# A hybrid decoder step: sums of the norms on one engine, the convolution's mean behind each tile, and a later write of the next layer's input

## The chip, the cores and the metric

The kernel runs on one core of one Trainium2 chip. A core has five engines that run side by side, each with its own in-order queue: TensorE (PE: matmul, with its weight loads shown as PEld), VectorE (DVE), ScalarE (ACT), GpSimd (POOL) and SyncE (SP, which here only issues DMAs). The metric is the device time of one execution in microseconds (us). Lower is better.

## The reference

One inference step of a two-layer decoder with width 1024: a prompt of 1024 tokens with 16 meta tokens ahead of it, and eight decode sequences of one token each. Layer 0 mixes tokens with a causal Conformer convolution, layer 1 with a recurrent mixer (RWKV-7). Each is followed by an MLP with 4096 hidden features. All is float32.

```python
hn  = rmsnorm(h, norm_mix[i])
# layer 0
u   = hn @ w_pw1 + b_pw1;  u = u[:D] * sigmoid(u[D:])
c   = depthwise_conv(u, w_dw) + b_dw            # 31 taps along time
mu  = mean(c);  var = mean((c - mu)**2)         # over the 1024 features
cn  = (c - mu) * rsqrt(var + LN_EPS) * ln_g + ln_b
out = silu(cn) @ w_pw2 + b_pw2
# both layers
h   = h + out
h   = h + square(relu(rmsnorm(h, norm_mlp[i]) @ w_in)) @ w_out
```

What matters here are the means over the 1024 features of a token: the mean and the variance of the layer norm, and the mean square of each RMS norm.

## The kernel before, in words

Activations lie with features on the 128 partitions and tokens along the free axis, so the 1024 features are KT = 8 tiles. Layer 0 works on the 1048 token columns in three groups of 352, 348 and 348 (`G0`), the second half of layer 1 on groups of 328, 352 and 352 (`G2`).

A matmul in float32 accuracy is three passes (`mm3`, L187 to L189): weights and activations are split into a high part in fp32r, cast by ScalarE (L157, L140), and a low part, the difference (L162 for weights, mostly on GpSimd, in four pieces of 256 columns each; L141 for activations).

A mean over features needs a sum over the 8 tiles and then one over the 128 partitions. The sum over tiles is done by additions on VectorE and GpSimd. `mean_bcast` (L231) does the rest: for every partial sum in a list it issues one float32 matmul with a matrix of 1/1024, all into one PSUM bank `st_...`, so that every partition holds the mean. There are two ways to sum over tiles:

- `mean_parts` (L223): GpSimd adds tiles 0, 2, 4, 6, VectorE tiles 1, 3, 5, 7; two partial sums. For a variance ScalarE squares each tile first (L218) into buffers with the tag `t1`. Used for the layer norm's mean (`mu`) and variance (`va`) and for the final norm.
- `square_sums` (L242, L253): called once per tile as it becomes ready; ScalarE squares, the engines named in a list add in turn, and the last two squares go into the list of parts as they are. With two engines there are four parts, with one engine three. Used for the norm ahead of each MLP (`m0` in layer 0, `m1` in layer 1) and for layer 1's input norm (`d`, whose first two groups have GpSimd alone already).

The stages that the change touches, in layer 0:

- `pw1(g)` computes `u`; `conv(g)` (L492) does the 31 taps for two tiles at a time on VectorE, 15 emission steps for a pair, in PSUM, and ScalarE copies the pair back over `u` (L509). `ln_silu(g)` (L555) is the layer norm: mean, subtraction (L563), variance, factor `rs` (L258, L260), product (L572), SiLU, split. Its output feeds `pw2(g)`, with PSUM tiles `ps_o`.
- `post(g)` does `pw2(g)`, the sums `m0`, and the first MLP of the group. While that MLP is emitted, a `filler` interleaves other work with it: `norm_out(g-1)`, `conv(g+1)` and `ln_silu(g+1)`, one after the other.
- `norm_out(g)` (L587) stores `h` to DRAM, sums its squares, forms the factor, multiplies `h` by it on VectorE (L602, eight instructions) and stores the product as layer 1's input, `d_hn` (L605). For the third group it runs after all else in the layer. Layer 1 reads it back as `hx` (L785, L787) and begins with differences `xx` (L791).

In the MLP (`mlp`) the first product's result in PSUM (`ps_in`) is multiplied with the norm's factor on VectorE (`r`, L327), squared (`s`, L329), split (`hh`, `hl`), multiplied by the second matrix (`out`), and added to `h` by VectorE (L340). The MLP's input (`m_h`, `m_l`, L269 and L270) does not contain the factor, so the matmuls may start before the norm is known; five PSUM banks (tag `mm`) hold results.

What sets the order: a generator yields a number when a piece of work has been emitted, and `filler` hands the pieces out evenly over the calls of `fill()`, of which an MLP has 192. `yield MW` (6) keeps the place of six pieces free. The counts beside the generators (for example `15 * KT // 2 + 2 + 2 * MW + KT`) are the number of such units. The emission order is a priority only: the tile scheduler simulates a timeline and gives each engine the ready instruction of the earliest emission, so an engine with nothing else to do may run work that was emitted much later. The resulting order in each engine's queue is fixed in the program.

The tags matter where buffers are few: `t1` has three buffers and is shared by the squares of the variance, `sg` in `pw1` and `r` in the MLP; the squares of `m1` have three buffers (`sq`); `acc0` and `acc1` have one each.

## Time and profile before

| | |
|---|---|
| median of three runs | 2878.38 us |
| the three runs | 2867.08, 2878.38, 9711.41 us |
| the profiled execution: its own time | 2870.67 us |
| its span, first to last instruction | 2869.0 us |
| mean granted TensorE clock | 0.961 |
| HBM read, written | 353.03 MB, 72.66 MB |

The span is what the views of the profile divide up; the 1.7 us between it and the execution's time lie outside any instruction. Layer 0 takes the first 1130 us or so, the recurrent mixer up to about 1900, its output projection and the first MLP group up to about 2370, and the MLP of the other two groups the rest. A row of the timeline reads: start, duration, engine, line, operation, output <- inputs, shape, count of merged instructions, and in brackets how long the engine was idle before it and what ended that. Durations of matmuls overlap, so their pace is read from start to start. A row of the waits reads: who waited, for whom, total us, times, longest.

### The profile page before, as it was taken

The page shows a single profiled execution, that of the slowest core. Times are in us where ns is not written, and L with a number is a line of the kernel's source. Part 1 is how long each engine was busy: PE and PEld are TensorE (multiplying, and loading weights), DVE is VectorE, ACT ScalarE, POOL GpSimd, SP SyncE. Part 2 cuts the span into 40 slices and gives each one's busy share as a digit, 9 for nine tenths or more (in the row PEclk, how much of TensorE's full clock was granted, in tenths as well). Part 3 has the DMA queues.
Part 4 walks back from the last instruction along what each step waited for, and adds up shares of the span by engine and source line. Part 5 has one row for each costly group of instructions (what it writes and reads, how often), then busy time and mean ns, then how long its engine had stood idle before and what let it go on. Part 6 is the DMA issues. An engine that isn't in the chain of part 4 may idle for free. (4 is left out here: it accounts for less than half of the span.)

```text
span 2869.0 us, 54486 instructions
## 1 busy us (share of the span) xinstructions
PE 2690.9 (94%) x20554; PEld 2567.2 (89%) x20554; DVE 1962.3 (68%) x3794; ACT 1350.6 (47%) x2515; POOL 1703.3 (59%) x2295
## 2 busy tenths in 40 slices
PE   8999999999999898878799889889999999999998
PEld 8998999999999898867678788778889999999998
DVE  5999999995455546377986885689656764443444
ACT  5545444544354334464666766634445552222223
POOL 6677877887788775444433463656438783433432
PEclk9999999999999999888999999989989999999999
DMA  6662544454444542676788877766556742222211
GB/s 176 178 187 88 155 134 133 138 177 136 140 130 142 175 140 89 201 208 178 200 210 217 236 188 184 204 175 161 134 150 206 205 136 85 67 74 67 67 60 41
DMA packets 659285, 428.34 MB, mean 149 GB/s; under 512 B 126840, under 2 KB 609208, under 8 KB 659022
## 3 DMA queue, kind: packets, MB, share of 16 engines
q1 hardware_dynamic: 652780, 421.93, 52.4%
q10 hardware_dynamic: 6018, 2.89, 0.4%
q8 instruction: 162, 2.65, 0.4%
q14 instruction: 101, 0.83, 0.1%
q0 software_dynamic: 224, 0.03, 0.0%
HBM read 353.03 MB, written 72.66 MB: 148 GB/s over the span
## 5 line engine op out<-in xcount | busy, mean ns | idle before, releaser
L162 POOL TENSOR_TENSOR wo_lo<-wo_raw,wo_hi 128x256 fp32r<-128x256 f32 x736 | 564.1, 800 | 281.8 <-ACT wo_hi L157 269.0
L162 POOL TENSOR_TENSOR wi_lo<-wi_raw,wi_hi 128x256 fp32r<-128x256 f32 x640 | 491.5, 800 | 278.4 <-ACT wi_hi L157 266.3
L187 PE MATMUL out<-hh,wo_hi 128*128 128x352 f32 (+2 forms) x1536 | 504.0, 328 | 20.1 <-DVE h L340 10.9
L340 DVE TENSOR_TENSOR h<-h,out 128x352 f32<-128x352 f32 (+2 forms) x768 | 385.8, 509 | 196.8 <-PE out L189 196.2
L187 PE MATMUL ps_in<-m_h,wi_hi 128*128 128x352 f32 (+2 forms) x1536 | 498.3, 325 | 10.3 <-ACT m_h L269 8.3
L188 PE MATMUL out<-hh,wo_lo 128*128 128x352 f32 (+2 forms) x1536 | 499.5, 325 | 0.0
L189 PE MATMUL out<-hl,wo_hi 128*128 128x352 f32 (+2 forms) x1536 | 495.5, 325 | 4.2 <-DVE hl L141 4.2
L188 PE MATMUL ps_in<-m_h,wi_lo 128*128 128x352 f32 (+2 forms) x1536 | 497.2, 324 | 0.0
L189 PE MATMUL ps_in<-m_l,wi_hi 128*128 128x352 f32 (+2 forms) x1536 | 496.2, 323 | 0.0
L504 DVE SCALAR_TENSOR_TENSOR cv<-u,wdw,cv 128x352 f32<-128x352 f32 (+2 forms) x720 | 376.5, 572 | 0.7
L157 ACT CAST wi_hi<-wi_raw 128x1024 fp32r<-128x1024 f32 x160 | 168.1, 1050 | 392.9 <-PE out L189 187.6
L157 ACT CAST wo_hi<-wo_raw 128x1024 fp32r<-128x1024 f32 x184 | 192.9, 1049 | 313.8 <-PE out L189 146.6
L187 PEld LDWEIGHTS out<-hh,wo_hi 128*128 128x128 f32 x1536 | 292.8, 191 | 27.5 <-DVE h L340 14.8
L187 PEld LDWEIGHTS ps_in<-m_h,wi_hi 128*128 128x128 f32 x1536 | 290.6, 189 | 13.6 <-ACT m_h L269 8.4
L189 PEld LDWEIGHTS out<-hl,wo_hi 128*128 128x128 f32 x1536 | 291.9, 191 | 6.5 <-DVE hl L141 5.5
L188 PEld LDWEIGHTS out<-hh,wo_lo 128*128 128x128 f32 x1536 | 292.8, 191 | 1.6
L188 PEld LDWEIGHTS ps_in<-m_h,wi_lo 128*128 128x128 f32 x1536 | 290.7, 189 | 2.0
L189 PEld LDWEIGHTS ps_in<-m_l,wi_hi 128*128 128x128 f32 x1536 | 290.2, 189 | 1.5
L327 DVE SCALAR_TENSOR_TENSOR r<-ps_in,rs_m 128x352 f32<-128x352 f32 (+2 forms) x192 | 98.6, 515 | 234.1 <-PE ps_in L189 230.5
L141 DVE TENSOR_TENSOR hl<-s,hh 128x352 fp32r<-128x352 f32 (+2 forms) x192 | 144.4, 753 | 111.8 <-ACT hh L140 111.6
L329 ACT ACTIVATE s<-r 128x352 f32<-128x352 f32 (+2 forms) x192 | 93.8, 490 | 134.6 <-DVE r L327 134.4
L162 POOL TENSOR_TENSOR wv_lo<-wv_raw,wv_hi 128x256 fp32r<-128x256 f32 x96 | 79.9, 864 | 25.9 <-ACT wv_hi L157 25.6
(403 smaller groups left out, 6195.0 us busy)
## 6 DMA issues: line engine op xcount, KB each, us to landing
wi_raw<-in_w_mlp_in_dram SPq DMA_DIRECT2D x160, 512.0 KB, 4.1
wo_raw<-in_w_mlp_out_dram SPq DMA_DIRECT2D x160, 512.0 KB, 3.7
wr_raw<-in_rwkv_w_r_dram SPq DMA_DIRECT2D x32, 512.0 KB, 6.0
wk_raw<-in_rwkv_w_k_dram SPq DMA_DIRECT2D x32, 512.0 KB, 5.6
wv_raw<-in_rwkv_w_v_dram SPq DMA_DIRECT2D x32, 512.0 KB, 5.4
d_ab<-ab SPq DMA_DIRECT2D x32, 512.0 KB, 3.3
pg_raw<-in_conv_w_pw_dram SPq DMA_DIRECT2D x24, 512.0 KB, 5.1
pa_raw<-in_conv_w_pw_dram SPq DMA_DIRECT2D x24, 512.0 KB, 4.5
```

Of the source, the lines that this page charges most:

```text
L141: eng_lo.tensor_sub(lo, src, hi.bitcast(F32))
L157: nc.scalar.copy(hi[:, :a * b], raw[:, :a * b])
L162: eng_lo.tensor_sub(lo[:, cs], raw[:, cs], hi[:, cs].bitcast(F32))
L187: nc.tensor.matmul(ps, w[0], act[0], start=first, stop=False)
L188: nc.tensor.matmul(ps, w[1], act[0], start=False, stop=False)
L189: nc.tensor.matmul(ps, w[0], act[1], start=False, stop=last)
L327: nc.vector.scalar_tensor_tensor(r[:, :n], ps[:, :n], 0.0, rs[:, :n], op0=ALU.max, op1=ALU.mult)
L329: nc.scalar.activation(s[:, :n], r[:, :n], AF.Square)
L340: nc.vector.tensor_add(hv[:, 4 * i + m, :], hv[:, 4 * i + m, :], ps[:, :n])
L504: nc.vector.scalar_tensor_tensor(acc[m][:, :n], ug[:, m, j:j + n], wdw[:, m, j:j + 1], acc[m][:, :n], op0=ALU.mult, op1=ALU.add)
```

## The change

It does five things. (1) `conv` itself emits the GpSimd additions for the layer norm's mean, tile by tile behind each pair's copy, into a tile with the tag `acc1`; tiles 6 and 7 are not added, they go into the list of parts. (2) In `ln_silu` the squares for the variance are emitted behind each tile's subtraction, and GpSimd adds all of them but the last, which goes to TensorE as it is. (3) `square_sums` gets GpSimd alone in every place where it had two engines: the third group's `d`, all `m0` and all `m1`. (4) In `norm_out` the multiplications come `MW` units after the factor in place of one. (5) In `ln_silu` ten units (`VW`) in place of six lie between the variance's sums and their matmul, and the counts follow. The final norm keeps `mean_parts`.

```diff
+            ln_sums = {}
+
             def conv(g):
 
                 n, ug = prompt_of(g), u[g]
+                n0, c = G0[g][1], u[g][:, :, CB:]
...
                     for m in ms:
                         nc.scalar.copy(ug[:, m, CB:CB + n], acc[m][:, :n])
+                    if pair == 0:
+                        tot = stat(f"acc_mu{g}", "acc1", 1)[:, :n0]
+                    if pair < KT - 2:
+                        for m in ms[not pair:]:
+                            nc.gpsimd.tensor_add(tot, tot if m > 1 else c[:, 0, :n0], c[:, m, :n0])
+                    else:
+                        ln_sums[g] = [tot] + [c[:, m, :n0] for m in ms]
...
             MW = 6
+            VW = 10
...
             def ln_silu(g):
                 n = G0[g][1]
                 c = u[g][:, :, CB:]
-                parts = mean_parts(c, n, f"mu{g}", False)
                 yield MW
-                mu = mean_bcast(parts, n, f"mu{g}")
+                mu = mean_bcast(ln_sums[g], n, f"mu{g}")
                 yield 1
+                tot = stat(f"acc_va{g}", "acc0", 1)
                 for k in range(KT):
                     nc.vector.tensor_sub(c[:, k, :n], c[:, k, :n], mu[:, :n])
-                yield 1
-                parts = mean_parts(c, n, f"va{g}", True)
-                yield MW
-                rs = rstd_of(mean_bcast(parts, n, f"va{g}"), n, 1, f"ln{g}")
+                    sq = tt(f"sq_va{g}{k}", "t1") if k else tot
+                    nc.scalar.activation(sq[:, :n], c[:, k, :n], AF.Square)
+                    if 0 < k < KT - 1:
+                        nc.gpsimd.tensor_add(tot[:, :n], tot[:, :n], sq[:, :n])
+                    if k % 4 == 3:
+                        yield 1
+                yield VW
+                rs = rstd_of(mean_bcast([tot, sq], n, f"va{g}"), n, 1, f"ln{g}")
                 yield 1
...
-                    add, parts = square_sums(n, f"d{g}", lambda k: tt(f"sqd{k}", "t1")[:, :n], (nc.gpsimd, nc.vector))
+                    add, parts = square_sums(n, f"d{g}", lambda k: tt(f"sqd{k}", "t1")[:, :n], (nc.gpsimd,))
                 for k in range(KT):
                     add(k, hv[:, k, :])
                     yield MW / KT
                 rs = rstd_of(mean_bcast(parts, n, f"d{g}"), n, 0, f"d{g}")
-                yield 1
+                yield MW
...
-                add, sums = square_sums(n, f"m0{g}", lambda k: u[g][:, k, :n], (nc.gpsimd, nc.vector), True)
+                add, sums = square_sums(n, f"m0{g}", lambda k: u[g][:, k, :n], (nc.gpsimd,), True)
...
                     gens.append(ranked(CV, norm_out(g - 1)))
-                    cnt += KT + 1 + MW
+                    cnt += KT + 2 * MW
                 if g < 2:
                     gens += [ranked(CV, conv(g + 1)), ranked(LN, ln_silu(g + 1))]
-                    cnt += 15 * KT // 2 + 2 + 2 * MW + KT
+                    cnt += 15 * KT // 2 + 4 + MW + VW + KT
...
                 return square_sums(n, f"m1{g}", lambda k: cur["tmp"].tile([P, cur["n"]], F32, name=f"sq{g}_{k}", tag="sq", bufs=3)[:, :n],
-                                   (nc.gpsimd, nc.vector))
+                                   (nc.gpsimd,))
```

The filler of `conv(0)` and `ln_silu(0)`, which runs beside `pw1`, gets the same new count (`15 * KT // 2 + 4 + MW + VW + KT`).

More of the change, by code (lines that the diff above doesn't have):

```diff
@@ L634, in hybrid_step @@
                 xin = pool(s, "xin", 3)
-                fill, rest = filler(8 * KT, ([ranked(CV0, conv(0)), ranked(CV0, ln_silu(0))], EARLY * (15 * KT // 2 + 2 + 2 * MW + KT)))
+                fill, rest = filler(8 * KT, ([ranked(CV0, conv(0)), ranked(CV0, ln_silu(0))], EARLY * (15 * KT // 2 + 4 + MW + VW + KT)))
                 for g in range(2):
```

## The prediction

> **What bounds the kernel now.** I read the page's busy shares first, then the busy time of four stretches (layer 0, the recurrent mixer, its output projection with the first MLP group, the last MLP), then the waits of TensorE, and then the timeline around each wait that names a norm.
>
> ```profile
> PE 2690.9 (94%) x20554; PEld 2567.2 (89%) x20554; DVE 1962.3 (68%) x3794; ACT 1350.6 (47%) x2515; POOL 1703.3 (59%) x2295
> ...
> 0.00:1130.00 1130.00, 1083.96 (x6676) 1066.96 (x6677) 841.01 (x1603) 522.73 (x798) 865.38 (x1188) 0.98 0.50 146
> 1130.00:1900.00 770.00, 666.10 (x7208) 599.95 (x7206) 572.16 (x1138) 465.71 (x1082) 344.10 (x488) 0.91 0.76 201
> 1900.00:2370.00 470.00, 451.13 (x3586) 411.81 (x3585) 332.64 (x646) 226.11 (x416) 315.61 (x382) 0.96 0.58 161
> 2370.00:2869.00 499.00, 489.70 (x3090) 488.46 (x3088) 216.50 (x407) 136.06 (x219) 178.21 (x238) 0.99 0.22 66
> ```
>
> In the stretches the columns are length, then busy PE, PEld, DVE, ACT, POOL, then the granted clock. TensorE (PE) is the bound in every stretch. Its idle time is 1130 - 1084 = 46 us in layer 0, 770 - 666 = 104 us in the recurrent stage, where none of the edited sums lies but the end of the last input norm's, and 470 - 451 = 19 us around the second mixer's output. So even a change that emptied every gap near the edited norms could win at most 46 + 19 = 65 us. Which of these gaps belong to the norms, the waits of PE say (total, times, longest):
>
> ```profile
> PE out L187 <- DVE r L327: 8.5, 4, 7.5
> PE ps_in L187 <- ACT m_h L269: 8.3, 1, 8.3
> PE st_mu L231 <- DVE acc_mu L223: 5.9, 1, 5.9
> PE ps_o L189 <- POOL ln_l L141: 2.1, 1, 2.1
> PE st_va L231 <- POOL acc_va L223: 2.1, 1, 2.1
> PE st_m L231 <- POOL acc_m L253: 1.4, 1, 1.4
> PE st_d L231 <- POOL acc_d L253: 0.6, 1, 0.6
> ```
>
> The four waits for `acc` tiles sum to 10 us; the first two lines are waits that the norms cause indirectly (below). The 5.9 us is the clearest:
>
> ```profile
> 199.96 0.45 ACT L509 COPY u<-cv 128x352 f32<-128x352 f32 x1 [4.89 <-DVE cv L504]
> 199.95 2.83 POOL L162 TENSOR_TENSOR pa_lo<-pa_raw,pa_hi 128x256 fp32r<-128x256 f32 x4
> ...
> 208.24 2.76 POOL L162 TENSOR_TENSOR pg_lo<-pg_raw,pg_hi 128x256 fp32r<-128x256 f32 x4
> 200.94 10.43 DVE L223 TENSOR_TENSOR acc_mu<-acc_mu,u 128x352 f32<-128x352 f32 x1
> 204.78 0.75 PE L231 MATMUL st_mu<-acc_mu,ones_d 128*128 128x352 f32 x2
> 211.43 1.54 PE L231 MATMUL st_mu<-acc_mu,ones_d 128*128 128x352 f32 x2 [5.90 <-DVE acc_mu L223]
> 212.25 1.01 PE L187 MATMUL ps_g<-hn_h,pg_hi 128*128 128x348 f32 x1
> ...
> 214.48 0.32 PE L187 MATMUL ps_g<-hn_h,pg_hi 128*128 128x348 f32 x1
> 214.64 0.32 PE L188 MATMUL ps_g<-hn_h,pg_lo 128*128 128x348 f32 x1
> 219.89 3.52 DVE L563 TENSOR_TENSOR u<-u,st_mu 128x352 f32<-128x352 f32 x8
> ```
>
> The last convolution tile is copied out by 200.41. Two engines had summed four tiles each; VectorE's last addition then takes 10.43 us, until 0.4 us after GpSimd's four batches of weight splits have ended at 211.0. PE had already issued the other half's matmul at 204.78 and stands still in order.
>
> **The change part by part.** *Additions moved.* Per layer norm the mean goes from 3 GpSimd and 3 VectorE additions to 5 and 0 (two tiles go to PE as they are), the variance from 3 and 3 to 6 and 0; each MLP norm (three in each layer) and the last input norm go from 2 and 2 to 5 and 0. GpSimd gets 3x2 + 3x3 + 7x3 = 36 more, VectorE loses 3x3 + 3x3 + 7x2 = 32. The two lines of additions, VectorE before GpSimd, show them all but the untouched final norm:
>
> ```profile
> 0.00:1200.00 1200.00, 25.35 (x18) 17.35 (x18) 0.97 0.50 146
> 0.00:2869.00 2869.00, 15.33 (x14) 22.54 (x24) 0.96 0.53 149
> L223 DVE TENSOR_TENSOR acc_mu<-acc_mu,u x6: 511/894/10433, 161.4 to 659.5; 128x348 f32<-128x348 f32 x4, 128x352 f32<-128x352 f32 x2
> ```
>
> VectorE loses 25.35 + 15.33 = 40.7 us. GpSimd pays 39.89/42 = 0.95 us for one, so 36 x 0.95 = 34 us more. GpSimd is idle for 1130 - 865 = 265 us of the first stretch and 470 - 316 = 154 us of the third, so the 34 us cost nothing where its weight splits run ahead of their use; where they do not, an addition puts its 0.95 us in front of PE. The Trainium skill speaks against the move: "GPSIMD Engine Reference", section 3.1, has a two-input addition on GpSimd at about twice VectorE's time. The rows agree on the price (0.95 against 0.51 for the shortest above), and by the rule alone the kernel would pay 36 x 0.95 - 32 x 0.51 = 18 us; the 10.43 us row says that VectorE's price is not 0.51 where GpSimd is busy.
>
> *Matmuls of the sums.* Parts per statistic: each mean 2 to 3; the last input norm and six MLP norms 4 to 3; variances and the first two input norms stay. Net 3 - 7 = -4.
>
> ```profile
> 1939.19 1.27 PE L231 MATMUL st_m<-acc_m,ones_d 128*128 128x328 f32 x4
> 1940.30 1.27 PE L231 MATMUL st_m<-sq,ones_d 128*128 128x328 f32 x4
> ```
>
> Two parts take 1.11 us from start to start, 0.56 each at 328 columns, 0.6 at 352: -2.4 us on PE itself.
>
> *First mean.* After, PE needs the copies of 200.41 and a GpSimd sum over tiles 0 to 5, of which the last is ready a convolution pair earlier. PE came at 204.78, so the 5.9 us goes; with it the slow matmuls behind the gap (six from 212.25 to 214.48, 2.23 us where six at 0.16 take 0.96, and the pair's 0.82 for 0.6), 1.5 us. Bounds: 0 if the last GpSimd addition falls behind the batches that start at 199.95, -7.4 otherwise. I take -7.4. What is late next is the subtraction at 219.89; VectorE's queue behind the 10.43 us moves up by the same time, so it follows.
>
> *Variance.* Six additions one after another in place of two chains of three, each with a batch of splits possibly ahead of it, and the squares rotate through three shared buffers:
>
> ```profile
> 223.82 3.11 POOL L162 TENSOR_TENSOR pa_lo<-pa_raw,pa_hi 128x256 fp32r<-128x256 f32 x4
> 2321.06 18.77 POOL L162 TENSOR_TENSOR wo_lo<-wo_raw,wo_hi 128x256 fp32r<-128x256 f32 x24
> ```
>
> From -2.1 (the wait goes) to 3 x (0.95 + 3.11) = +12.2 for the first group. The ten units of filler work in place of six before PE is asked make room for the longer chain, so I take 0, near the lower end. In the MLP norms three more additions have the same ends, or worse behind the 18.77 us batch; their result is first needed after five matmul banks have filled, and PE shows one wait of 1.4 us for them now. Taken 0.
>
> *Second mixer's first norm.* Its squares have three buffers, and ScalarE stands behind them:
>
> ```profile
> 1918.08 9.96 POOL L162 TENSOR_TENSOR wi_lo<-wi_raw,wi_hi 128x256 fp32r<-128x256 f32 x12
> 1925.65 1.01 DVE L253 TENSOR_TENSOR acc_m<-sq,sq 128x328 f32<-128x328 f32 x1
> 1926.70 0.84 ACT L242 ACTIVATE sq<-h 128x328 f32<-128x328 f32 x2 [7.70 <-DVE acc_m L253]
> ```
>
> The 8.3 us wait for `m_h` comes from this late VectorE addition. On GpSimd it may run before the 9.96 us batch or behind it: -8.3 to +10. I take 0.
>
> *Next layer's input later.* Eight VectorE multiplications and the store of `d_hn` behind them (SP queue) come six units after the norm's factor, not one.
>
> ```profile
> L605 SPq DMA_DIRECT2D d_hn<-h x3: 513/525/546, 608.8 to 1144.3; - x3
> 972.52 6.76 DVE L602 SCALAR_TENSOR_TENSOR h<-h,pvec,rs_d 128x348 f32<-128x348 f32 x8
> 979.20 5.36 DVE L791 TENSOR_TENSOR xx<-hx 128x272 f32<-128x272 f32 x6
> 984.49 0.51 DVE L327 SCALAR_TENSOR_TENSOR r<-ps_in,rs_m 128x348 f32<-128x348 f32 x1
> 985.14 0.63 PE L187 MATMUL out<-hh,wo_hi 128*128 128x348 f32 x1 [7.48 <-DVE r L327]
> 1128.51 0.91 POOL L253 TENSOR_TENSOR acc_d<-acc_d,sqd 128x348 f32<-128x348 f32 x1
> 1151.40 0.13 POOL L1039 MEMSET n<- 128x32 f32 x1 [8.91 <-DMA d_hn<-h]
> ```
>
> The eight were emitted one per unit and still ran back to back: the planner fills VectorE with whatever is ready, and this run of 6.76 + 5.36 us delayed `r`, for which PE waited 7.5 us. The later emission may part the two runs (-7.5) or make the same wait elsewhere (+7.5). Readiness and not emission placed them, so 0. Of the three stores (608.8 to 1144.3, 0.5 us of SP queue each, moved behind a few weight loads) only the last has a waiter that the profile shows. After the last group nothing fills, so the wait adds nothing there, but three more GpSimd additions stand before the store that GpSimd itself waits for at 1151.40: 0 to 3 x 0.93 = 2.8, taken 1.
>
> **Sum.** The profiled run took 2870.67 us, 1.7 around its span of 2869.0. 2870.67 - 2.4 - 7.4 + 1 = 2861.9, so 2862. That is 16 us (0.6%) below the median of the three runs shown, 2878.38, whose lowest is 2867.08. Two per cent, 57 us, is about what a measurement of this kernel can tell from no change.
>
> **Rivals.** *Hidden.* PE passes the mean earlier, but the second projection (`ps_o`, 2.1 us wait now) then waits for `ln_l` by as much, because VectorE still does the subtraction behind the next group's convolution. Only -2.4 and +1 are left: 2869. For it: that wait exists. Against: VectorE's queue itself moves up. The Trainium skill, "Perfetto Trace Analysis", section "Optimizing Scalar/DVE Operations", says that offloading between GpSimd and VectorE might not help as they share a read port; it points to this time, while the 10.43 us row points to the other.
>
> *GpSimd late once per norm.* Ten statistics (three variances, six MLP norms, the last input norm) each find the chain one batch late, 2.76 us: +28, 2890. For: three waits of this kind stand in the list with only half the additions.
>
> *GpSimd in the path throughout* (the other side). Every added addition stands behind a batch while its square's buffer holds up ScalarE, and so the weight casts that GpSimd waits for: 36 x (0.95 + 2.76) = 134, 2996. It eats the gain of 8.8 from the third addition on, and passes 2% when 18 of 36 do it (57 + 9 = 66 us). Against: GpSimd is 59% busy.
>
> *More waits go*: 2.1 + 2.1 + 1.4 + 7.5 + 8.3 = 21 us further, 2841. *The planner's order changes everywhere*, and half of the 104 us of the recurrent stage goes: 2862 - 52 = 2810. For: one order is planned for the whole kernel. Against: nothing edited lies there.
>
> **How the numbers follow.** Forecast 0.36, hidden 0.19, late once per norm 0.19, more waits go 0.12, GpSimd throughout 0.09, order everywhere 0.05. The first four lie within 2%: same 0.86, faster 0.05, slower 0.09. They reach from 2841 to 2890, with a little for spread at the lower end 2840. The forecast alone I would put at 2850 to 2872.
>
> **What would show it.** Right: no `st_mu` wait on VectorE, 36 more GpSimd additions near 0.95 us, `st_va` waits under 4 us, `hl` and `h` of VectorE unchanged. Wrong: `st_va`, `st_m` or ScalarE's squares waiting for GpSimd for over 20 us in total, or a difference that lies between 1130 and 1900.

## The result, and the profile after

The kernel before took 2872.73 us (median of 4 runs beside those of the changed kernel), the changed one 2915.81 us (median of 4): a ratio of 1.0162, with a 95% interval of 1.0140 to 1.0185. One of the four runs of the kernel before took 9711.41 us and has no part in the ratio, which goes by the fast runs alone; so the ratio, and not the 43 us between the medians, gives the cost: 1.62%, about 46 us. That is within 2%, the class that the prediction thought likeliest, but on the slower side, and above the range's upper end of 2890.

The profiled execution of the changed kernel took 2928.55 us (span 2926.8), the longest of its four (the others: 2912.84, 2915.15 and 2916.46). Its trace therefore shows 57.8 us where the ratio gives 46; places and mechanisms are read from traces, sizes from the ratios.

The page's busy line of the changed kernel:

```profile
PE 2711.5 (93%) x20546; PEld 2580.4 (88%) x20546; DVE 1927.5 (66%) x3762; ACT 1351.0 (46%) x2517; POOL 1723.6 (59%) x2331
```

The instructions moved as they were counted: VectorE (DVE) has 32 fewer (3794 to 3762), GpSimd (POOL) 36 more (2295 to 2331), TensorE (PE) 8 fewer rows. GpSimd is still only 59% busy. The busy times of the same four stretches of work (the limits moved by 33.6, 39 and 54 us, as the matmuls around them did), with the columns of the prediction's table:

```profile
0.00:1163.60 1163.60, 1094.91 (x6674) 1073.38 (x6674) 808.03 (x1577) 522.34 (x797) 877.02 (x1213) 0.97 0.48 142
1163.60:1939.00 775.40, 659.22 (x7160) 596.61 (x7161) 567.07 (x1132) 467.22 (x1085) 348.52 (x490) 0.91 0.75 199
1939.00:2424.00 485.00, 463.82 (x3625) 418.05 (x3624) 335.93 (x647) 225.46 (x416) 319.44 (x392) 0.96 0.56 156
2424.00:2926.80 502.80, 493.55 (x3092) 492.32 (x3090) 216.48 (x407) 135.97 (x219) 178.64 (x238) 0.99 0.22 66
```

Layer 0 is 33.6 us longer (1130 to 1163.6), the recurrent stage 5.4, the stretch with the second mixer's output and the first MLP group of layer 1 15, the last MLP 3.8. (The second limit lies inside the recurrent work. From its first matmul, `p_r`, to the first `ps_in` behind it that work takes the same time in both kernels, 803.4 and 803.6 us, so the 5.4 us there are won back ahead of the MLP.) In layer 0 TensorE's idle time grew by 23 us (46 to 68.7) and its busy time by 11. So the loss lies in the stretches that hold edited sums, and most of it in layer 0. The waits of TensorE in the changed kernel (total, times, longest):

```profile
PE out L187 <- DVE h L340: 19.5, 9, 7.5
...
PE st_m L231 <- POOL u L253: 9.8, 2, 5.6
...
PE ps_in L189 <- DVE m_l L270: 8.4, 2, 8.2
PE ps_a L187 <- ACT sg L481: 8.3, 1, 8.3
...
PE out L187 <- ACT hh L140: 7.4, 5, 3.2
PE p_g L187 <- ACT hxh L140: 7.2, 1, 7.2
```

Two waits of the kernel before are gone, the 5.9 us of `st_mu` for VectorE and the 7.5 us of `out` for `r`. New or longer are `st_m` for GpSimd (1.4 us before), `ps_a` for `sg`, `p_g` for `hxh`, `out` for `hh` (0.6 before) and the largest, `out` for `h` (10.9 before, no single one above 2.3).

How a norm's sum gets late can be read at one place, the first MLP norm of layer 0. GpSimd's timeline in the changed kernel (start, length, instruction, in brackets the idle time before it):

```profile
262.97 9.56 POOL L162 TENSOR_TENSOR p_lo<-p_raw,p_hi 128x256 fp32r<-128x256 f32 x12 [5.52 <-ACT p_hi L157]
272.49 1.09 POOL L253 TENSOR_TENSOR u<-u 128x352 f32<-128x352 f32 x1
273.55 6.19 POOL L162 TENSOR_TENSOR wi_lo<-wi_raw,wi_hi 128x256 fp32r<-128x256 f32 x8
279.70 0.94 POOL L253 TENSOR_TENSOR u<-u 128x352 f32<-128x352 f32 x1
280.60 5.92 POOL L162 TENSOR_TENSOR wi_lo<-wi_raw,wi_hi 128x256 fp32r<-128x256 f32 x8
...
287.24 0.80 POOL L253 TENSOR_TENSOR u<-u 128x352 f32<-128x352 f32 x1
288.00 2.84 POOL L162 TENSOR_TENSOR wo_lo<-wo_raw,wo_hi 128x256 fp32r<-128x256 f32 x4
290.81 0.95 POOL L253 TENSOR_TENSOR u<-u 128x352 f32<-128x352 f32 x1
291.72 2.83 POOL L162 TENSOR_TENSOR wo_lo<-wo_raw,wo_hi 128x256 fp32r<-128x256 f32 x4
294.52 2.77 POOL L162 TENSOR_TENSOR wi_lo<-wi_raw,wi_hi 128x256 fp32r<-128x256 f32 x4
...
298.12 0.80 POOL L253 TENSOR_TENSOR u<-u 128x352 f32<-128x352 f32 x1
```

The squares that these five additions (L253) take were made by ScalarE between 264.70 and 280.65. The five together last 4.6 us, yet they are spread over 26 us, since each stands in GpSimd's one queue behind four to twelve pieces of weight splits (L162), and the chain is serial. (At both places marked `...` stands an addition for the next group's mean, which part (1) of the change put there.) What the chain's end releases, in the changed kernel:

```profile
294.44 0.32 PE L189 MATMUL ps_in<-m_l,wi_hi 128*128 128x352 f32 x1
298.98 3.88 PE L231 MATMUL st_m<-u,ones_d 128*128 128x352 f32 x6 [4.21 <-POOL u L253]
303.51 1.03 PE L550 MATMUL pcs<-ident,u 128*30 128x128 f32 x4 [0.65 <-ACT sd_m L258]
...
309.75 0.66 PE L187 MATMUL out<-hh,wo_hi 128*128 128x352 f32 x1
...
303.49 2.35 DVE L260 RECIPROCAL rs_m<-sd_m 128x352 f32<-128x352 f32 x1 [0.22 <-ACT sd_m L258]
...
306.65 1.38 DVE L327 SCALAR_TENSOR_TENSOR r<-ps_in,rs_m 128x352 f32<-128x352 f32 x3
```

and the same in the kernel before:

```profile
297.30 0.32 PE L187 MATMUL out<-hh,wo_hi 128*128 128x352 f32 x1
...
289.40 2.34 DVE L260 RECIPROCAL rs_m<-sd_m 128x352 f32<-128x352 f32 x1
...
292.55 0.94 DVE L327 SCALAR_TENSOR_TENSOR r<-ps_in,rs_m 128x352 f32<-128x352 f32 x2
```

Both kernels begin this MLP at nearly the same time (first `ps_in` at 278.6 and 279.3). In the changed one TensorE has filled the banks by 294.8 and then has nothing that may run: the first bank is read by `r` at 306.65, 14.1 us later than before, and `out` starts 12.5 us later. Before, `r` read the first bank at 292.55, some 2 us before the changed kernel's TensorE ran out of banks: that was all the slack there was.

The stop costs more than its 4.21 us. Behind it the granted clock is 0.50, and the `st_m` matmuls follow one another at 0.59 us in place of 0.30. The first row is the changed kernel's stretch of `st_m`, the second that of the kernel before, in the columns of the stretches above:

```profile
298.90:303.30 4.40, 3.88 (x6) 1.84 (x6) 4.37 (x9) 0.40 (x1) 4.40 (x8) 0.50 0.49 132
285.80:288.40 2.60, 2.60 (x12) 1.75 (x11) 2.60 (x6) 0.00 (x0) 2.60 (x5) 1.00 0.53 159
```

At the second group the sum is late too, and the wait has another name. The factor `rs_m` starts at 604.66 us, 25 us later than before (579.70), where the group's MLP itself starts 15.5 us later. VectorE then has eight subtractions of the layer norm and the eight products for layer 1's input in front of `h` (all between 611.48 and 622.10), and TensorE's `out` waits 7.54 us for `h` at 622.58. That is the longest wait of the first line.

### The profile page after: what moved, and what is told of

Same layout as the page of the kernel before. It is cut to its first block, busy times and chain, and to the rows that moved or that the text cites. A ratio compares the mean times of both kernels' runs of the same rounds, so it can differ in the third digit from the quotient of the medians.

```text
span 2926.8 us, 54569 instructions
## 1 busy us (share of the span) xinstructions
PE 2711.5 (93%) x20546; PEld 2580.4 (88%) x20546; DVE 1927.5 (66%) x3762; ACT 1351.0 (46%) x2517; POOL 1723.6 (59%) x2331
## 4 chain that ended last, share of the span: by engine, by line
PE 32%; DVE 7%; POOL 6%; issue 3%; ACT 2%; DMA 2%; SPq 0%; DVEq 0%; POOLq 0%; ACTq 0%
POOL wo_lo L162 3%; PE out L187 3%; PE out L188 3%; PE out L189 3%; PE ps_in L187 3%; PE ps_in L188 3%; PE ps_in L189 3%; POOL wi_lo L162 2%; PE A L1221 2%; DVE ni L1181 1%; DVE tt L1180 1%; PE p_k L187 1%; PE p_k L188 1%; PE p_k L189 1%; PE U L1303 1%
## 5 line engine op out<-in xcount | busy, mean ns | idle before, releaser
L162 POOL TENSOR_TENSOR wo_lo<-wo_raw,wo_hi 128x256 fp32r<-128x256 f32 x736 | 558.9, 791 | 314.2 <-ACT wo_hi L157 292.9
L162 POOL TENSOR_TENSOR wi_lo<-wi_raw,wi_hi 128x256 fp32r<-128x256 f32 x640 | 484.5, 789 | 272.0 <-ACT wi_hi L157 268.1
L187 PE MATMUL out<-hh,wo_hi 128*128 128x352 f32 (+2 forms) x1536 | 507.3, 330 | 28.7 <-DVE h L340 19.5
L162 POOL TENSOR_TENSOR wv_lo<-wv_raw,wv_hi 128x256 fp32r<-128x256 f32 x96 | 82.7, 892 | 32.9 <-ACT wv_hi L157 22.1
```

Of the source, the lines that this page charges most:

```text
L162: eng_lo.tensor_sub(lo[:, cs], raw[:, cs], hi[:, cs].bitcast(F32))
L187: nc.tensor.matmul(ps, w[0], act[0], start=first, stop=False)
```

## Experiments

For every kernel the table has the ratio to the kernel before with its 95% interval, the median, and, of the profiled execution, the start of a few matmuls (the same matmul in every kernel): the first `out` of layer 0, the first `p_r` (the recurrent stage begins), the first `ps_in` of layer 1, and the end of the span. The kernel before was run anew beside every set of experiments (medians 2872.88 to 2875.48 us), and each ratio is to the runs of its own set, so it is not the quotient of two medians of this table.

| kernel | ratio | median us | first `out` | `p_r` | `ps_in` | end |
|---|---|---|---|---|---|---|
| before | 1 | 2872.73 | 297.3 | 1124.7 | 1928.1 | 2869.0 |
| after | 1.0162 (1.0140 to 1.0185) | 2915.81 | 309.7 | 1158.3 | 1961.9 | 2926.8 |
| e1_sums_back | 0.9974 (0.9959 to 0.9989) | 2868.42 | 297.7 | 1118.8 | 1918.5 | 2862.5 |
| e2_sums_only | 1.0175 (1.0153 to 1.0197) | 2925.01 | 313.6 | 1157.2 | 1961.5 | 2925.0 |
| e3_ln_only | 0.9995 (0.9980 to 1.0011) | 2874.11 | 294.7 | 1120.8 | 1922.6 | 2872.8 |
| e4_out_only | 1.0010 (0.9995 to 1.0025) | 2878.27 | 299.1 | 1118.2 | 1916.7 | 2876.0 |
| e5_m0_back | 1.0058 (1.0040 to 1.0077) | 2892.82 | 297.1 | 1121.0 | 1923.4 | 2892.5 |
| e7_four_to_pe | 1.0014 (1.0000 to 1.0027) | 2879.58 | 299.5 | 1121.9 | 1929.3 | 2881.5 |
| e8_vector_only | 0.9992 (0.9974 to 1.0010) | 2872.49 | 296.5 | 1119.4 | 1924.2 | 2871.8 |
| e9_var_vector | 0.9897 (0.9871 to 0.9924) | 2846.67 | 287.0 | 1104.1 | 1898.3 | 2836.6 |
| e10_m0_vector | 0.9960 (0.9946 to 0.9975) | 2860.78 | 282.0 | 1098.6 | 1921.4 | 2854.9 |
| e11_all_vector | 0.9989 (0.9976 to 1.0002) | 2868.73 | 286.0 | 1101.3 | 1916.5 | 2861.2 |
| e12_no_later | 0.9937 (0.9912 to 0.9962) | 2856.22 | 287.2 | 1111.7 | 1911.8 | 2855.1 |
| e13_m0_01_vector | 0.9970 (0.9957 to 0.9983) | 2865.68 | 284.8 | 1105.2 | 1904.4 | 2859.0 |

**The change taken apart.** e1_sums_back is the changed kernel with the squares' sums of the seven norms on both engines again; e2_sums_only is the kernel before with that edit alone; e3_ln_only has the layer norm's part alone, e4_out_only the later write alone.

```diff
 e1, against the changed kernel (e2 is the reverse, against the kernel before)
-add, parts = square_sums(n, f"d{g}", lambda k: tt(f"sqd{k}", "t1")[:, :n], (nc.gpsimd,))
+add, parts = square_sums(n, f"d{g}", lambda k: tt(f"sqd{k}", "t1")[:, :n], (nc.gpsimd, nc.vector))
-add, sums = square_sums(n, f"m0{g}", lambda k: u[g][:, k, :n], (nc.gpsimd,), True)
+add, sums = square_sums(n, f"m0{g}", lambda k: u[g][:, k, :n], (nc.gpsimd, nc.vector), True)
...
-                   (nc.gpsimd,))
+                   (nc.gpsimd, nc.vector))
 e4, against the kernel before
-                yield 1
+                yield MW
-                    cnt += KT + 1 + MW
+                    cnt += KT + 2 * MW
```

> The changed kernel, with the sums of the MLP norms and of the last input norm given back to GpSimd and VectorE in turn; the layer norm's new sums and the later write stay. Theory A (the serial GpSimd chain of these seven sums delays the norm's factor, the MLP's first matmuls fill their five banks, and TensorE stands): the aligned traces put +12 to +14 us on the first group's MLP start, +10 on the second, +8 net on the third, +20 on the second mixer's first group, so most of the 43 us between the medians goes: 2865 to 2880. Theory B (the layer norm's variance squares, whose three buffers are shared with the gate sg and with r, hold up ScalarE): the loss stays, 2900 to 2920. Theory C (the later write and the planner's order that follows from it): 2900 to 2920.

> The kernel before, with only the seven sums (MLP norms, last input norm) put on GpSimd alone; layer norm and the write of the next layer's input as before. Theory A: nearly the whole loss, 2900 to 2920. Theories B and C: no loss, 2865 to 2880.

> The kernel before, with only the layer norm's part of the change: mean behind each convolution pair, variance on GpSimd alone with ten units ahead of its matmul. Theory A: the 5.9 us wait for the mean goes, the 8.3 us wait for the gate's PSUM bank comes in its place, so 2865 to 2880. Theory B: 2900 to 2920. Theory C: 2865 to 2880.

> The kernel before, with only the later multiplications and write of the next layer's input (six units in place of one, and the count that goes with it). Theories A and B: about the time before, 2860 to 2880; by A the 7.5 us wait of TensorE for r near 985 us may move or go. Theory C: 2895 to 2920.

The seven sums alone cost what the whole change costs (1.0175 and 1.0162, with overlapping intervals), and without them the rest of the change is a little faster than the kernel before (0.9974). The time of e2, 2925, is 5 us above what theory A gave. The layer norm's part alone and the later write alone make no difference that these intervals can tell from none. So the loss is in the seven sums.

**Which sums, and what of them.** e5_m0_back puts the three sums of layer 0's MLP norms (m0) back on two engines and leaves the third decoder norm (d) and layer 1 (m1) on GpSimd.

```diff
-add, sums = square_sums(n, f"m0{g}", lambda k: u[g][:, k, :n], (nc.gpsimd,), True)
+add, sums = square_sums(n, f"m0{g}", lambda k: u[g][:, k, :n], (nc.gpsimd, nc.vector), True)
```

> The changed kernel with one sum put back: the three first-layer MLP norms (m0) have their adds on GpSimd and VectorE in turn again; the third decoder norm (d) and the second layer's MLP norms (m1) stay on GpSimd alone. Theory A (GpSimd's in-order queue delivers each of these norms' sums late, and TensorE stands once five banks are full): the shift against the kernel before grew to +33.6 us by the start of RWKV, nearly all of it at the m0 norms, so about 34 to 40 us come back: 2876 to 2884, no st_m wait on u of more than 2 us, and the start of RWKV at or before the kernel before's; the +16 to +20 us at the first m1 norm stay. Rival (the loss comes from the total load on GpSimd, wherever it is put): 15 of the 21 sums' adds that changed are back, the loss falls in proportion, and the m1 part falls too: about 2885 with the m1 part under 10 us. Rival C (planner's order): 2905 to 2916.

It came out at 1.0058, above what was expected. The place was right: the recurrent stage begins at 1121.0, before the kernel before's 1124.7, and no `st_m` wait on `u` is left. The remainder was too small: from e1 to e5 it is 1.0058 - 0.9974 = 0.84%, 24 us for m1 and d, not 16 to 20. The m0 sums cost 1.0162 - 1.0058 = 1.04%, 30 us. (The sum of 54 us exceeds the change's 46 because the rest of it gains 7.) The rival of e5, total load, was counted wrongly: of the 21 additions that the seven sums moved to GpSimd, m0 has 9 and not 15. In proportion 12/21 of 54, 31 us, would have stayed; 24 did, which by itself is not far enough off to exclude it. What speaks against it is e7, below. A small part of the 24 lies in the recurrent stage, where TensorE waits for the input that the third d norm writes, 5.7 us in this kernel, 7.2 in the changed one, and not at all in e1; net, the stage is 2.7 us longer than e1's (802.4 and 799.7 us from `p_r` to `ps_in`):

```profile
PE p_g L187 <- ACT hxh L140: 5.7, 1, 5.7
```

Between the kernel before and the changed one a larger part appears at the first m1 norm: the changed kernel lies 33.8 us behind at the first `ps_in` of layer 1, 52.0 at the 33rd `out` behind it and 54.0 at the 768th. GpSimd's timeline there, in the changed kernel:

```profile
1957.11 0.88 POOL L253 TENSOR_TENSOR acc_m<-sq,sq 128x328 f32<-128x328 f32 x1
1957.96 10.21 POOL L162 TENSOR_TENSOR wi_lo<-wi_raw,wi_hi 128x256 fp32r<-128x256 f32 x12
1968.14 0.99 POOL L253 TENSOR_TENSOR acc_m<-acc_m,sq 128x328 f32<-128x328 f32 x1
...
1982.91 3.06 POOL L162 TENSOR_TENSOR wo_lo<-wo_raw,wo_hi 128x256 fp32r<-128x256 f32 x4 [9.52 <-ACT wo_hi L157]
1985.93 1.31 POOL L253 TENSOR_TENSOR acc_m<-acc_m,sq 128x328 f32<-128x328 f32 x1
...
1993.44 1.06 POOL L253 TENSOR_TENSOR acc_m<-acc_m,sq 128x328 f32<-128x328 f32 x1
```

Five additions of about 1 us take 37 us from the first to the last. In the midst of them GpSimd stands idle for 9.52 us, in front of a split whose input ScalarE has not yet made: the addition behind it waits for that weight. Idle time on GpSimd is thus no proof that an addition put there is free.

Between e1 and e5, whose ratios give the 24 us, the same matmuls show it at another place: e5 lies 4.9 us behind e1 at the first `ps_in` of layer 1, 15.1 at the first `out`, only 5.5 at the 161st and 24.4 at the 293rd. From the 161st to the 293rd no edited sum runs, and TensorE does the same 1008 matmuls in every kernel, idle for 1.4 us at most. They take 82 us in e1, e9, e10 and e12, at a granted clock of 1.00, and 97 to 102 us in the ten others, at 0.91 to 0.97 (97.8 in the kernel before, 101.1 in the changed one, 101.2 in e5). So how much of the 24 us is the lateness of these sums is not settled.

e7_four_to_pe keeps GpSimd alone but sends four tiles' squares of each m0 and m1 norm straight to TensorE, not two, so that GpSimd adds three times per norm and not five; it also gives the squares of m1 four buffers, not three. e8_vector_only puts all seven chains on VectorE alone (the edit is shown for m0; d and m1 have the same).

```diff
 e7 (direct is 4 for m0 and m1, and 2 elsewhere)
-                if k >= KT - 2:
+                if k >= KT - direct:
...
-... tag="sq", bufs=3) ...
+... tag="sq", bufs=4) ...
 e8
-lambda k: u[g][:, k, :n], (nc.gpsimd,), True)
+lambda k: u[g][:, k, :n], (nc.vector,), True)
```

> The changed kernel, but in the m0 and m1 norms the last four feature tiles' squares go straight to TensorE in place of two: GpSimd adds three times per norm in place of five, TensorE multiplies two more 4-byte tiles (about 0.6 us each, 12 in all: +7 us at most). m1's squares have four buffers in place of three for it. Theory A: the last add of the first m0 norm comes two pitches of the queue (5 to 7 us each) sooner, the first `out` group starts near 299 us in place of 309.75, the st_m wait of 4 to 6 us goes, and the time is 2878 to 2898. Rival (one add behind a backlog costs as much as five, since all wait for the same batch of weight splits): st_m still waits for GpSimd, 2910 to 2923.

> The changed kernel, but the m0, third d and m1 sums run on VectorE alone: a chain of five adds as in the changed kernel, on the other engine, 36 more adds on VectorE and none of them on GpSimd. Theory A1 (what is late is GpSimd's queue, which stands behind weight splits): the sums are ready with the squares; 2858 to 2876, no st_m wait, first `out` group at or before 297.3 us. Rival A2 (what is late is a chain of five adds on any one engine in place of two shorter chains): 2895 to 2916. Rival A3 (VectorE is as crowded: its adds and subtractions for evictions come later by 5 x about 1 us per norm): a little over the kernel before, 2876 to 2890, with `out <- DVE h` waits above 15 us.

Both came out as the queue's lateness has it. With three additions the last one of the first m0 norm starts at 285.6 us, not 298.12, and the time falls by 1.0162 - 1.0014 = 1.5%, 43 us, though TensorE has more to do. Only 12 of the 21 additions were taken off GpSimd, 31 us of 54 in proportion, so more came back than the load's share. (How much of the 43 the fourth buffer of m1 gives was not tested apart.) With five on VectorE they are over in time. All additions of that norm in e8 (least, median and longest ns; first and last start):

```profile
L253 DVE TENSOR_TENSOR u<-u x5: 571/778/1055, 266.0 to 276.7; 128x352 f32<-128x352 f32 x5
```

and in the changed kernel:

```profile
L253 POOL TENSOR_TENSOR u<-u x5: 799/937/1091, 272.5 to 298.1; 128x352 f32<-128x352 f32 x5
```

In layer 0 a single chain of five is not at fault (rival A2), and one addition is not much dearer on GpSimd, 0.94 against 0.78 us; the last one begins 21 us later. VectorE's own queue bore the load in layer 0 (A3 falls). In layer 1 one wait of 4.2 us for VectorE's sum appeared, and there A2 has a part: from the second MLP group's first `ps_in` to the end, the five kernels whose m1 sums are chains of five take 518.5 to 519.7 us, on either engine (e8 and e11 on VectorE), and the nine others 514.3 to 515.1.

**Where the first mean's gain went.** e9_var_vector is e1 with the variance's additions on VectorE.

```diff
-                        nc.gpsimd.tensor_add(tot[:, :n], tot[:, :n], sq[:, :n])
+                        nc.vector.tensor_add(tot[:, :n], tot[:, :n], sq[:, :n])
```

> The kernel of the first set's best (the changed kernel with the seven squares' sums back on two engines, 0.9974 of the kernel before), with the variance's six adds per layer norm on VectorE in place of GpSimd. Theory B (the squares' three buffers are shared with sg, come free only as GpSimd adds between weight splits, and hold sg of the next group back): the wait of ps_a for sg, 8.3 us, falls below 2 us and the time is 5 to 8 us less than the kernel it is made from: 0.9950 of the kernel before, 2860 to 2863 where the kernel before has 2874. Rival (VectorE's six more adds stand ahead of its subtractions and evictions): ps_a or another wait of 5 us or more turns up on VectorE in the same place, and the time is within 3 us of the kernel it is made from. Rival (the wait is on the squares of ScalarE themselves): no change in the wait of ps_a for sg.

In the changed kernel ScalarE's squares wait for GpSimd, each time for one batch of splits, and behind the last of them stands `sg`, which takes its buffer from the same three (`t1`). The view is ScalarE's timeline:

```profile
216.66 0.50 ACT L576 ACTIVATE sq_va<-u 128x352 f32<-128x352 f32 x1 [2.25 <-POOL acc_va L578]
...
223.97 0.50 ACT L576 ACTIVATE sq_va<-u 128x352 f32<-128x352 f32 x1 [2.18 <-POOL acc_va L578]
...
227.59 0.55 ACT L481 ACTIVATE sg<-ps_g,pvec 128x348 f32<-128x348 f32 x1 [0.83 <-POOL acc_va L578]
```

and TensorE's next row is

```profile
228.19 0.66 PE L187 MATMUL ps_a<-hn_h,pa_hi 128*128 128x348 f32 x1 [8.29 <-ACT sg L481]
```

In e9 the squares come 1.7 us apart (215.25 to 216.94) in place of 3.7 (two, from 216.66 to 223.97), and `sg` 9 us sooner:

```profile
215.25 0.50 ACT L576 ACTIVATE sq_va<-u 128x352 f32<-128x352 f32 x1 [0.26 <-DVE acc_va L578]
...
216.94 0.50 ACT L576 ACTIVATE sq_va<-u 128x352 f32<-128x352 f32 x1 [1.19 <-DVE acc_va L578]
218.62 0.55 ACT L481 ACTIVATE sg<-ps_g,pvec 128x348 f32<-128x348 f32 x1 [1.19 <-DVE acc_va L578]
```

The 8.3 us wait is gone, and the first `out` starts 10.7 us before e1's, as theory B has it and a little more. Against e1, e9 is 0.9974 - 0.9897 = 0.77%, 22 us, faster, three times what was expected. In the profiled executions (e9's is the fastest of its four) 14.7 of 25.9 us are there when the recurrent stage begins; the other 11 come later, where nothing was edited, with most of the instructions but not all in the same order (3245 of TensorE's 3630 steps in the recurrent stage). (A step is a run of TensorE's instructions on the same tiles.) Theory B explains the first part only. e9 is the fastest of these kernels, 1.0% under the kernel before.

**The later write.** e12_no_later is e9 with the write of the next layer's input, and its count, as in the kernel before.

```diff
-                yield MW
+                yield 1
-                    cnt += KT + 2 * MW
+                    cnt += KT + 1 + MW
```

> The best kernel so far (0.9897 of the kernel before) without the later write of the next layer's input (yield of 1 and its count as in the kernel before). Theory C1 (the later write is what takes the 7.5 us stand of out for r on VectorE near 985 us away): that wait comes back and the time is 5 to 8 us more, 2851 to 2856. Rival C2 (the stand goes because everything ahead of it is earlier): no such wait, within 3 us of 2847.

The wait came back. TensorE's timeline in e12:

```profile
972.24 0.63 PE L187 MATMUL out<-hh,wo_hi 128*128 128x348 f32 x1 [7.38 <-DVE r L327]
```

What delays `r` in e12, on VectorE:

```profile
959.74 7.18 DVE L617 SCALAR_TENSOR_TENSOR h<-h,pvec,rs_d 128x348 f32<-128x348 f32 x8
966.84 4.83 DVE L806 TENSOR_TENSOR xx<-hx 128x272 f32<-128x272 f32 x6
971.59 0.51 DVE L327 SCALAR_TENSOR_TENSOR r<-ps_in,rs_m 128x348 f32<-128x348 f32 x1
```

and the same run in e9:

```profile
934.99 2.33 DVE L260 RECIPROCAL rs_d<-sd_d 128x348 f32<-128x348 f32 x1
...
939.73 4.78 DVE L617 SCALAR_TENSOR_TENSOR h<-h,pvec,rs_d 128x348 f32<-128x348 f32 x8
```

The write that is to come later comes 20 us earlier. The edit also raises the stream's count from KT + 1 + MW to KT + 2 * MW, and the filler advances all of the stream faster for it: the norm's own factor `rs_d` comes at 934.99 in e9 and at 956.3 in e12, 84.1 and 105.9 us after the start of the third MLP. There the stream is `norm_out` alone and its count goes from 15 to 20 (15/20 = 0.75, 84.1/105.9 = 0.79). In the second MLP, where the same five units come on top of 103, the factor comes 24.5 and 24.6 us after the start. So it is the count. The run of VectorE then misses the moment at which TensorE needs `r`. Theory C1 holds: 7.6 us in the trace when the recurrent stage begins, and 0.9937 - 0.9897 = 0.40% (11 us) in the ratios, with intervals that just overlap. In e4 the wait went as well (2.9 us of `out` for `r` in all, 8.5 in the kernel before) and the factor came 21 us earlier, but the time did not fall.

**Towards a better version.** e10_m0_vector is e9 with the m0 sums on VectorE alone, e11_all_vector has those of d and m1 there as well, and e13_m0_01_vector only those of the first two m0 norms.

```diff
 e13, against e9 (e10: without the condition)
-add, sums = square_sums(n, f"m0{g}", lambda k: u[g][:, k, :n], (nc.gpsimd, nc.vector), True)
+add, sums = square_sums(n, f"m0{g}", lambda k: u[g][:, k, :n], (nc.vector,) if g < 2 else (nc.gpsimd, nc.vector), True)
```

> The best kernel so far (the changed kernel with the seven squares' sums on two engines and the variance's adds on VectorE, 0.9897 of the kernel before), with the first layer's three MLP norms (m0) summed on VectorE alone. Theory (whatever of a norm's sum is still on GpSimd is late by its queue): with all on VectorE the first MLP group ended 6 us earlier against the kernel before than with two engines (-1.8 to +4.5 us), the second 3 us earlier; so 3 to 6 us less than the kernel it is made from, 2840 to 2844 where the kernel before has 2873. Rival (VectorE now carries the variance's adds too and is the engine that ends last): 2847 to 2856, with more waits of out for h on VectorE than its 9.0 us.

> As the run before it, and the third decoder norm and the second layer's MLP norms (m1) are summed on VectorE alone too: no norm's sum has an instruction on GpSimd but those of the layer norm's mean. With all sums on VectorE and the variance on GpSimd the stretch of the first m1 group cost 6.4 us more against the kernel before (-3.8 to +2.6 us between its first and its second matmul group, -9.5 to -6 with two engines overall). Theory (in m1 VectorE is behind with the states' and the residual's work, so that there two engines are better): 4 to 8 us more than e10_m0_vector. Rival (VectorE's queue is nowhere as late as GpSimd's): the same as e10_m0_vector or 3 us less.

> The best kernel so far (0.9897 of the kernel before, built from the changed kernel) with the first two MLP norms (m0 of groups 0 and 1) summed on VectorE alone and the third, like m1, on two engines. e10_m0_vector, which has all three on VectorE, was ahead by 5.4 us at the start of RWKV and behind by 23.1 us at its end; in that stretch the order of its instructions differs from that of the kernel it is made from (2776 of 3603 steps of TensorE stand in the same order), here it is nearly the same (3535 of 3603). Theory P (the planner's other order of the RWKV stage, not the sums' engine, is what e10 lost): the gain of about 5 us at the start of RWKV is kept through it, RWKV lasts 794 to 802 us from the first p_r to the next MLP in place of e10's 823, and the time is 2838 to 2846. Rival V (the sums on VectorE cost later, by whatever is pushed back on it): RWKV lasts 812 us or more, and the time is 2853 to 2865.

e10 missed. It is 5.4 us ahead of e9 when the recurrent stage begins, as the theory has it, and 23.1 us behind when it ends (822.8 us in place of 794.2), with no longer waits of `out` for `h` (8.9 and 9.0 us), so its rival is nearer in the number (2856 at most; it took 2860.78) but has the wrong place. In that stage 2791 of TensorE's 3630 steps stand in the same order as in e9. e11 fell 8 us behind e10, with a wait of 9.0 us of `st_m` for VectorE's sum (the theory's upper end). e13 was chosen because its order in the recurrent stage is nearly e9's (3562 of 3630 steps), and there it lasts 799.2 us, as theory P has it. But its lead of 4.4 us at the second MLP group was gone before that stage, and between the first and the 769th `ps_in` of layer 1 it lost 16 us (439.6 and 423.3 us), so its time is the rival's, without the rival's place. Nearly all of it is lost in the piece named at e5: e13 lies 7.2 us behind e9 at the 161st `out` of layer 1 and 24.1 at the 293rd, over the same 1008 matmuls and with no idle time. Part of this is the granted clock (the number behind the engines' busy times). In e13:

```profile
2041.00:2139.70 98.70, 98.70 (x1009) 80.64 (x1009) 47.27 (x104) 40.64 (x85) 40.67 (x54) 0.97 0.47 121
```

and in e9:

```profile
2033.70:2115.60 81.90, 81.90 (x1010) 71.96 (x1009) 47.52 (x106) 40.63 (x84) 39.40 (x51) 1.00 0.57 147
```

By an estimate from these rows, 0.03 of 98.7 us, some 3 us of the 17 are the clock's; the others are not explained. Why the lead goes in layer 0, and what sets the clock and the pace in that piece, stays open: no run separates them.

## Why the prediction was wrong, step by step

*The step that failed* is the MLP norms: "their result is first needed after five matmul banks have filled, and PE shows one wait of 1.4 us for them now. Taken 0", together with "the 34 us cost nothing where its weight splits run ahead of their use". Both halves of the condition were looked at in the wrong row. A short wait says that the sum is in time, not how much later it could be; the room was about 2 us at the first m0 norm (292.55 against the banks' end), and the serial chain moved the last addition by 14 us. And the price of an addition on GpSimd is not its 0.95 us but its place in the queue: 26 us for 4.6 us of additions at m0, 37 us at m1. I had priced this place once per norm, as the rival of 2890, with one batch of 2.76 us each, though I had quoted a batch of 18.77 us. The runs put the m0 sums at 30 us and m1 with d at 24, where the sum had 0 and 1 (e1, e5), and e7 and e8 showed that it is GpSimd's queue that makes the m0 sums late, and the more so the longer its chain. For m1 with d the 24 us stand by e1 and e5, but only the changed kernel's own trace puts most of them at the sum.

*First mean, -7.4.* The wait went: `st_mu` starts at 200.70 us without one. The gain did not arrive: the first `ps_in` of the MLP starts 0.7 us later than before. "VectorE's queue behind the 10.43 us moves up by the same time, so it follows" was true of VectorE, but the next late thing is `sg`, through the variance's buffers.

*Variance, 0 between -2.1 and +12.2.* Mis-sized: with its additions on GpSimd it costs the whole gain of the mean, 8.3 us of `ps_a` in the first group. The prediction named the shared buffers but looked for the cost at `st_va` alone, whose wait did vanish, and not at the others that use them. The rival *hidden* had the right outcome for this part with the wrong place (`ps_o` for `ln_l`). What speaks for it in the Trainium skill, "Perfetto Trace Analysis", section "Optimizing Scalar/DVE Operations", that moving work between GpSimd and VectorE might not help, does not decide it here: the same additions took 1.7 us a step on VectorE in e9 and 3.7 us on GpSimd, by the queue they stood in.

*Matmuls, -2.4.* The count was right (8 fewer rows, two for each float32 matmul); nothing else tells its size.

*Second mixer's first norm, 0 between -8.3 and +10.* Wrong side: the wait for `m_h` moved to `m_l` (8.2 us) and the factor came later, since the chain stood behind a batch of 10.21 us and an idle 9.52. (The move from `m_h` to `m_l` alone is not the chain's doing: e3, e4 and e9, with two engines there, have it too, at 5.4 to 7.2 us.)

*Next layer's input later, 0 between -7.5 and +7.5.* It is the lower end in e9, where e12 shows the 7.4 us wait back without it; in e4 the wait goes and the time stays. "Readiness and not emission placed them" is half of it: the eight start within 2.5 us of their factor's end in both e9 and e12, but emission placed the factor, 21 us earlier with the raised count.

*Last input norm, +1.* About right in the end: TensorE waits 7.2 us for `hxh` in the recurrent stage, and not in e1 or e8, but of the 5.7 us of e5 only 2.7 are left at the stage's end.

The signs given beforehand mostly did their work. Of those for being right, the `st_mu` wait on VectorE went, the 36 more GpSimd additions came and `st_va` stayed under 4 us, but VectorE's `h` did not stay unchanged (10.9 to 19.5 us). The sign of failure, `st_m` or ScalarE's squares waiting for GpSimd for over 20 us in total, came: the rows have 9.8 + 1.9 us for `st_m` and 11.0 for the variance's squares, 22.7, and 15.1 more for the squares of m1. The rival *order everywhere* has no part in the loss where it was put, as the recurrent stage lasts 803.4 us before and 803.6 after from `p_r` to `ps_in`, though its order changed; but between e9 and e10 it was worth 28.6 us.

## What to carry to other kernels

An instruction put on an engine costs, for those who wait for it, its place in that engine's queue, backlog and idle waits included; read the timeline of that engine at the very place, and count a serial chain as its length times that pitch. Slack behind a sum is read from the time at which the consumer runs out of other work, not from the smallness of the present wait. Where squares, gates and other tiles share a few buffers, a slower reader of one of them holds back all; and an edit to a filler's counts moves all of the stream, not only the step that it is meant for.

## What the runs showed of the hardware that I had not expected

The 10.43 us of a VectorE addition beside GpSimd, on which the first mean's price rested, is neither the rule nor alone. Most are short: the variance's additions on VectorE in e9 took 0.51 to 0.91 us and those of m0 in e8 0.51 to 1.06, nearly all beside GpSimd's splits. But every kernel here has one to five VectorE instructions of over 3.3 us, each over a time in which GpSimd hardly pauses. In the kernel before:

```profile
2340.68 5.62 POOL L162 TENSOR_TENSOR wi_lo<-wi_raw,wi_hi 128x256 fp32r<-128x256 f32 x8
2341.30 5.38 DVE L253 TENSOR_TENSOR acc_m<-sq,sq 128x352 f32<-128x352 f32 x1 [2.74 <-ACT sq L242]
```

This addition ends 0.4 us after GpSimd's batch, as the one of 10.43 us did. What picks out these few is not shown.

TensorE is slower after it has stood: in the changed kernel the six `st_m` matmuls behind the 4.21 us gap took 0.79 to 0.95 us each where the eight of the kernel before took 0.46, and a transposition group of `pcs` 1.03 us where it took 0.60. The granted clock there is 0.50, against 1.00 before. It was so at each of the four longest waits of the changed kernel's layer 0 (8.29, 7.54, 5.59 and 4.21 us): the clock goes to 0.50 some 2 to 4 us after TensorE stopped, and stays there for 7 to 14 us. In layer 0 as a whole TensorE's busy time rose by 11 us along with 23 us of idle time.

The recurrent stage lasted between 794.2 and 822.8 us from `p_r` to the next `ps_in` in kernels whose edits lie elsewhere; with the order the same in every step but one, e9 and e12 were 5.9 us apart (794.2 and 800.1). A profile's single difference of that size in such a stage proves nothing about an edit.
